# Aligned pads in SBUF and a new order of the first block's loads and tiles in a split-fp32 transformer layer

## The chip, the core and the metric

The kernel runs on one core of a Trainium2 chip. The core has a matrix engine (TensorE, PE in the profile; PEld is its loading of the stationary operand), VectorE (DVE), ScalarE (ACT), GpSimd (POOL) and SyncE (SP), which here issues nearly all transfers, and 16 DMA engines. Operands lie in SBUF, 128 partitions wide; TensorE accumulates into PSUM banks. The metric is the device time of one execution in microseconds; a comparison uses the median of several runs.

## What is computed

One layer over 2048 prompt tokens and 128 sample tokens (8 streams of 16), model width 1024, all in fp32:

```python
qm, km, vm, om, ip, fp, qa, ka, va = split_in(x @ w_in)          # 1024 -> 2824
...
hm, C1, n1, m1 = mlstm_chunkwise(qm, km, vm, logi, logf, C0, n0, m0, mchunk)
hm = (og * head_norm(hm, g_mlstm_norm)).reshape(B, T, M_WIDTH).astype(x.dtype)
qa = rope(qa.reshape(B, T, A_Q_HEADS, A_HEAD_DIM), pos)
ka = rope(ka.reshape(B, T, A_KV_HEADS, A_HEAD_DIM), pos)
...
mix = jnp.concatenate([hm, ha], axis=-1) @ w_out
h = layer_norm(DEEPNORM_ALPHA * x + mix, ln1_g, ln1_b)
f, conv_rows = conv_ffn(h, conv_prev, w_up, w_conv, b_conv, w_down)   # 1024 -> 5632 -> 2816 -> 1024
y = layer_norm(DEEPNORM_ALPHA * h + f, ln2_g, ln2_b)
```

The gates ip, fp and the keys and values ka, va make up 264 columns of the input projection; the other 2560 are five groups of 512.

## The kernel before

**How a product is made.** Every fp32 operand is split in two: a high half, made by a cast on ScalarE, and a low half, source minus high half, on VectorE (`split`, lines 217 and 218 for weights, 562 and 563 for x). TensorE multiplies high by high, high by low and low by high and adds them in PSUM. On top of it the large matrix products use a scheme of seven quadrant products in place of eight, so sums and differences of quadrants of x and of the weights have to be formed on VectorE first (`x_steps` for x, steps named t1 to t4, and `split_first` for the weights of the first block), and the results are combined after (`i_after`).

**Stages.** The input projection (`i_dense`) runs in four blocks of four tiles of 128 tokens, the first block with the sample tile as a fifth; it lies at 6 to some 655 us of the span, with mLSTM and attention steps of finished tiles woven in between. The output projection follows, then the up-projection with the convolution (line 1842 its matmuls, 384 or 320 columns wide, some 940 to 1890 us) and the down-projection with the last norm (line 2045, to the end).

**An order written by hand.** TensorE executes in the order of the program, which is a list of items, made in `i_begin`. An item ("p", b, g, s) is product s (1 to 7) of group g in block b: 24 matmuls of 256 columns (line 700), and in the first block, for s of 1, 2, 5 and 4, 12 more for the sample tile (line 710, PSUM tile psx). An item ("t", b, i, e) is a direct tile: the 264 columns for tile i of block b, 24 matmuls of 264 columns (line 726), not done by quadrants. For groups 0 and 1 the split x (`oh`, `ol`) is the moving operand and the weights stationary; for the later ones, as in the direct tiles, it is the other way round. Before, block 0 runs tiles 2, 3 and 4 first, then products (0,0,1), (0,0,2), (0,1,1), (0,0,7), (0,0,6), (0,0,5) and on; tiles 0 and 1 come at the block's end, ahead of tiles 2 and 3 of block 1, whose x is loaded and split during the last group.

**Loads and splits.** The weights and x come by DMA, issued from SP in program order. `next_raw` issues the next weight load if one of four raw slots is free; `next_split` splits the oldest loaded one into halves; `advance` does either as long as it can. A quadrant of weights or x is 512 KB. `x_load(0, q)` loads quadrant q of block 0's x: 1 and 3 hold the two halves of the model width for tiles 0 and 1, 2 and 4 those for tiles 2 and 3 (called x1 to x4 below; product 1 uses x1, product 2 uses x3, direct tiles 2 and 3 use x2 and x4); `xs` is the sample tile. The order of loads before is x2, the four parts of the 264 columns' weights (`wg`, 264 KB each), x4, xs, the rotary tables, x1, four quadrants of group 0, x3, a quadrant of group 1. Some sums of weight quadrants are kept in DRAM (`zws`) for the later blocks.

**After a direct tile** (`i_keys`): ScalarE copies keys, values and gates out of PSUM, VectorE turns the keys (rotary steps, lines 864 to 867), SP stores them. When all tiles of a block have their gates, `gate_logs` computes the log-sigmoid in sixteen small VectorE operations; in block 0 that is after tile 1, thus after the block's end, and block 1's first x splits are issued there too.

**Addresses.** Pools are laid out one behind the other in a partition. In the kernel before, the x tiles and their halves (pool `xp`) begin at 96 bytes past a multiple of 512, the up-projection's inputs (`hh1` to `hh7`, `hl1` to `hl7`, made in `f_tokens`) at 480, 96 or 128, the down-projection's features at 480 and 96. The weight halves begin at 192 and 320.

Of the kernel before, what the change touches and what calls it, by code (L numbers as in the profile page):

```python
# [14 lines left out]
P = 128  # L15
# [189 lines left out]
class Prog:  # L205
# [8 lines left out]

    def split(self, hi, lo, src):
        nc = self.nc
        nc.scalar.copy(hi, src)  # L217
        nc.vector.tensor_sub(lo, src, hi.bitcast(F32))  # L218
# [7 lines left out]
    def run(self):  # L226
        PS = bass.MemoryType.PSUM
        nb = len(OBLOCKS)
        with ExitStack() as es:
# [20 lines left out]
            wx, wxcm = enter("wx1sb")  # L250
            self.unit_more(wx)
# [31 lines left out]
            self.wx, wxcm = enter("wx2sb")  # L283
            self.f2, f2cm = enter("f2sb")
            self.f3, f3cm = enter("f3sb")
            self.f_ups(n)
            close(f3cm)
# [47 lines left out]
    def i_begin(self):  # L335
# [3 lines left out]
        for b in range(nb):  # L339
            if b == 0:  # L340
                it += [("t", 0, i, -1) for i in (2, 3, 4)]
                it += [("p", 0, 0, s) for s in (1, 2)] + [("p", 0, 1, 1)] + [("p", 0, 0, s) for s in (7, 6)]
# [16 lines left out]
            it += [("t", b, i, b) for i in (0, 1)]  # L359
# [60 lines left out]
    def next_raw(self):  # L420
# [5 lines left out]
        there = u[0] == "p" and u[1] == 0 and (u[2] == 0 and u[3] != 1 or u[3] in (5, 4, 3) or u[2:] == (1, 1))  # L426
        if not there and not self.kept(u) and not self.raw_free():
            return False
# [24 lines left out]
        elif u[0] == "g":  # L453
            self.raw_of[u] = e = self.raw_slot([P, 2, 264])
# [36 lines left out]
    def split_first(self, g, s, hi, lo):  # L491
# [9 lines left out]
        if s == 7:  # L501
            V.tensor_sub(r[a11], r[a11], r[a21])
            keep(a11, 7)
        elif s == 6:
# [3 lines left out]
            keep(a11, 6)  # L508
        q = {1: a11, 7: a11, 6: a11, 2: a12, 3: a12, 5: a21, 4: a22}[s]
# [5 lines left out]
        if g >= KEPT and s in SUMS:  # L515
            for i, t in enumerate((hi, lo)):
                nc.sync.dma_start(self.zws[g][SUMS.index(s)][i].rearrange("p a b -> p (a b)"), t.bitcast(F32))
        if s == (6 if g == 0 else 2):
# [17 lines left out]
    def x_steps(self, b, *steps):  # L536
# [3 lines left out]
        for s in steps:  # L540
# [14 lines left out]
            else:  # L555
# [3 lines left out]
                n = 4 if (b, s) == (0, "b12") else 1  # L559
# [18 lines left out]
    def i_first_weights(self):  # L578
        for q in ((0, 0), (1, 0), (1, 1), (0, 1)):
            self.raw_of[0, q] = self.raw_slot([P, 4, HT])  # L580
        for q in ((0, 0), (0, 1), (1, 0), (1, 1)):
            self.nc.sync.dma_start(self.raw_of[0, q][0], self.a["wi"][0][q])

    def i_dense(self):
# [3 lines left out]

        self.next_raw()
        self.x_load(0, 2)  # L590
        for _ in range(3):
            self.next_raw()
        self.x_load(0, 4)
        self.single_raw = self.tp.tile([P, KD, P], F32, name="xsr", tag="pth", bufs=2)
        nc.sync.dma_start(self.single_raw, a["xs"])
        self.angles = {}
        self.rope_load(IBLOCKS[0][2], 2)
        self.rope_load(NPT, 1)
        self.next_split()
        self.x_steps(0, "b12")  # L600
        for _ in range(3):
            self.next_split()
        self.x_steps(0, 3)
# [1533 lines left out]
```

## Time and profile before

| | us |
|---|---|
| median of 3 runs | 2361.76 (2360.01 to 2362.44) |
| the profiled execution | 2359.6 |
| its span | 2357.8 |
| TensorE busy | 2316.6 |
| VectorE busy | 1805.4 |
| ScalarE busy | 1297.9 |

The mean granted clock of TensorE is 0.997. The span is what lies between the first and the last recorded instruction. In a group's row the name left of the arrow is the tile written, those to its right the tiles read (for a matmul the moving operand and then the stationary one); then come the shapes, the count, the busy time and the mean duration of one, and the idle time ahead of it with what ended it. A matmul's duration is longer than the distance from one start to the next, because matmuls overlap; for a stream of them the distance counts. In a timeline row the first two numbers are start and length.

### The profile page before, as it was taken

How to read it: one execution, taken by the hardware profiler on the slowest of the kernel's cores; microseconds unless marked ns; L12 is line 12 of the kernel's file. 1: busy time of each engine (PE TensorE's matmuls, PEld its weight loads, DVE VectorE, ACT ScalarE, POOL GpSimd, SP SyncE). 2: the span in 40 equal slices, each digit the busy share in tenths (PEclk: the TensorE clock that was granted, in tenths of full speed). 3: DMA queues.
4: the chain of work that ended last, by engine and by line, in shares of the span. 5: the costliest groups of instructions: out<-in, count | busy, mean ns of one | idle time of the engine just before them, and what ended most of it. 6: DMA issues, size and time to landing. Idle time of an engine off the chain costs nothing.

```text
span 2357.8 us, 39882 instructions
## 1 busy us (share of the span) xinstructions
PE 2316.6 (98%) x14425; PEld 2123.4 (90%) x14425; DVE 1805.4 (77%) x3150; ACT 1297.9 (55%) x2465; POOL 243.4 (10%) x298
## 2 busy tenths in 40 slices
PE   8999999999999999999999999999999999999998
PEld 7999998999987777999999999999999978888876
DVE  8677586796678888987788677768766776795897
ACT  5353466676666664655556555555554544554643
POOL 0101101101212221300001000002100100000100
PEclk9999999999999999999999999999999999999999
DMA  7788899889977657787777989887988786757653
GB/s 278 263 308 291 282 290 313 285 289 319 301 259 247 210 208 251 264 324 277 281 270 252 309 314 318 303 271 263 321 286 265 230 283 203 240 186 226 233 181 108
DMA packets 296933, 624.98 MB, mean 265 GB/s; under 512 B 47004, under 2 KB 140192, under 8 KB 296736
## 3 DMA queue, kind: packets, MB, share of 16 engines
q1 hardware_dynamic: 295872, 619.29, 77.3%
q10 hardware_dynamic: 864, 3.15, 0.4%
q8 instruction: 114, 1.87, 0.3%
q14 instruction: 83, 0.68, 0.1%
HBM read 451.78 MB, written 170.56 MB: 264 GB/s over the span
## 4 chain that ended last, share of the span: by engine, by line
PE 73%; DVE 5%; DMA 2%; issue 2%; ACT 2%; POOL 0%; SPq 0%; DVEq 0%; ACTq 0%; POOLq 0%
PE dps L1842 18%; PE fup L1842 18%; PE dps L700 7%; PE dps L2045 7%; PE fht L2045 6%; PE fup L2045 6%; PE dps L222 2%; PE dps L224 2%; PE dps L223 2%; PE ppo L1337 1%; PE psc L1288 1%; PE ppt L1331 1%; PE dps L726 1%; DVE w L218 1%; DVE hl L218 1%
## 5 line engine op out<-in xcount | busy, mean ns | idle before, releaser
L1842 PE MATMUL dps<-hh,uw 128*128 128x384 f32 (+1 forms) x1848 | 481.0, 329 | 6.7 <-ACT u L1867 1.9
L1842 PE MATMUL fup<-hh,uw 128*128 128x384 f32 (+1 forms) x1848 | 479.8, 328 | 2.7 <-ACT u L1867 2.6
L1842 PEld LDWEIGHTS dps<-hh,uw 128*128 128x128 f32 x1848 | 330.0, 188 | 10.5 <-ACT u L1867 2.7
L1890 DVE SCALAR_TENSOR_TENSOR cc<-u,cw,cc 128x768 f32<-128x768 f32 (+1 forms) x264 | 252.4, 977 | 107.5 <-ACT cc L1888 105.5
L1842 PEld LDWEIGHTS fup<-hh,uw 128*128 128x128 f32 x1848 | 330.1, 188 | 4.0 <-ACT u L1867 3.5
L1842 PE MATMUL fup<-hl,uw 128*128 128x384 f32 (+1 forms) x924 | 302.8, 328 | 1.6 <-DVE hl L218 1.6
L1842 PE MATMUL dps<-hl,uw 128*128 128x384 f32 (+1 forms) x924 | 302.4, 327 | 0.0
L700 PE MATMUL dps<-w,oh 128*128 128x256 f32 x1344 | 259.3, 286 | 2.8 <-ACT zev L759 1.0
L218 DVE TENSOR_TENSOR w<-wraw,w 128x1024 fp32r<-128x1024 f32 (+2 forms) x167 | 190.4, 1148 | 58.8 <-ACT w L217 58.1
L217 ACT CAST w<-wraw 128x1024 fp32r<-128x1024 f32 (+2 forms) x167 | 163.0, 985 | 129.1 <-PE dps L700 52.9
L217 ACT CAST uw<-wraw 128x1024 fp32r<-128x1024 f32 x126 | 122.9, 978 | 189.3 <-PE dps L2045 108.8
L700 PEld LDWEIGHTS dps<-w,oh 128*128 128x128 f32 x1344 | 213.1, 189 | 14.7 <-issue 8.9
L1888 ACT ACTIVATE cc<-u,cw 128x768 f32<-128x768 f32 (+1 forms) x132 | 129.6, 998 | 123.0 <-DVE u L1881 61.4
L218 DVE TENSOR_TENSOR uw<-wraw,uw 128x1024 fp32r<-128x1024 f32 x126 | 142.4, 1132 | 71.0 <-ACT uw L217 70.2
L700 PE MATMUL dps<-w,ol 128*128 128x256 f32 x672 | 189.6, 282 | 0.0
L700 PE MATMUL dps<-oh,w 128*128 128x256 f32 x896 | 171.1, 285 | 8.2 <-ACT dps L775 2.9
L1842 PEld LDWEIGHTS fup<-hl,uw 128*128 128x128 f32 x924 | 173.6, 188 | 2.5 <-DVE hl L218 2.5
L2045 PE MATMUL fup<-uw,fu 128*128 128x512 f32 x726 | 174.1, 396 | 1.6 <-DVE uw L218 1.6
L1842 PEld LDWEIGHTS dps<-hl,uw 128*128 128x128 f32 x924 | 173.6, 188 | 0.0
L2045 PEld LDWEIGHTS fup<-uw,fu 128*128 128x128 f32 x726 | 136.3, 188 | 34.9 <-DVE uw L218 2.1
L2045 PE MATMUL dps<-uw,fu 128*128 128x512 f32 x660 | 165.0, 396 | 0.0
L700 PEld LDWEIGHTS dps<-oh,w 128*128 128x128 f32 x896 | 140.9, 188 | 14.7 <-issue 4.1
(331 smaller groups left out, 4624.7 us busy)
## 6 DMA issues: line engine op xcount, KB each, us to landing
uw<-zw SPq DMA_DIRECT2D x176, 512.0 KB, 4.9
zw<-uw SPq DMA_DIRECT2D x88, 512.0 KB, 2.9
w<-zws SPq DMA_DIRECT2D x72, 512.0 KB, 6.6
wv<-wup SPq DMA_DIRECT2D x66, 512.0 KB, 5.5
wraw<-wi SPq DMA_DIRECT2D x65, 512.0 KB, 4.9
wraw<-zt SPq DMA_DIRECT2D x60, 512.0 KB, 4.1
wraw<-wdn SPq DMA_DIRECT2D x45, 512.0 KB, 3.7
wraw<-wo SPq DMA_DIRECT2D x40, 512.0 KB, 4.5
```

The costliest lines, as they stand in the source:

```text
L217: nc.scalar.copy(hi, src)
L218: nc.vector.tensor_sub(lo, src, hi.bitcast(F32))
L222: mm(out, ah, bh, start=start, stop=False)
L223: mm(out, ah, bl, start=False, stop=False)
L224: mm(out, al, bh, start=False, stop=stop)
L700: mm(o, l, r, start=s in (1, 7) and c == k == i == 0, stop=k == 3 and i == 2, skip_group_check=True)
L726: mm(o, x, w, start=k == i == 0, stop=k == KD - 1 and i == 2, skip_group_check=True)
L1288: nc.tensor.matmul(ps[kvh][:, j, :nk], q[rs, j0 + j], k[rs, sel], start=i == 0, stop=i == 2)
L1842: mm(ps, l[:, k], r[:, k], start=s in (1, 7) and k == 0 and i == 0, stop=k == 3 and i == 2, skip_group_check=True)
L1888: S.activation(c[:, v], u[:, v, 2:2 + n], AF.Identity, bias=w[3], scale=w[2])
L1890: V.scalar_tensor_tensor(c[:, v], u[:, v, i:i + n], w[i], c[:, v], op0=ALU.mult, op1=ALU.add)
L2045: mm(ps, l[:, k, c], r[:, k], start=s in (1, 4, 7) and u == 0 and k == 0 and i == 0, stop=u == nu - 1 and k == n - 1 and i == 2, skip_grou ...
```

## The change

It has two parts that do not depend on each other.

The first is the head. Block 0 now begins with products (0,0,1), (0,0,2) and (0,1,1); all five direct tiles follow, 0 to 4, then (0,0,7) and (0,0,6), and none is left at the block's end. The loads are issued in the order of that use: x1 and the first weight quadrant in halves by turns, the first half of the sample tile, the second quadrant, x3, the other half of the sample tile, group 1's quadrant, wg0, wg1, x2, wg2, wg3, x4 and the last two quadrants; the raw wg go to slots of the x pool (`oh5`, `ol5`, `oh6`, `ol6`) that are not needed yet. x1 is split in quarters, in place of x2. The first product does the first half of the inner dimension for both column halves before the second. The sums of group 0's weight quadrants for products 5 and 6 are formed after product 7's split, not ahead of product 6's. Steps that hung on tile 1 of block 0 (splits of x for block 1, the gate steps) are moved to other items.

The second is the addresses: `skew` allocates a tile that nothing writes or reads, ahead of or between pools, so that what follows begins at a multiple of 512 bytes. The small tiles of the norms are taken from another pool (`f2` in place of `wp`). The number of instructions of each engine stays, but for three more DMAs on SP.

```diff
+    def skew(self, pool, n):
+        pool.tile([P, n // 4], F32, name="skew", tag=f"skew{n}", bufs=1)
+
...
             wx, wxcm = enter("wx1sb")
+            self.skew(wx, 64)
             self.unit_more(wx)
...
             self.wx, wxcm = enter("wx2sb")
+            self.skew(self.wx, 64)
...
             self.f_ups(n)
+            self.skew(self.f2, 480)
+            self.skew(self.wx, 448)
...
-                it += [("t", 0, i, -1) for i in (2, 3, 4)]
-                it += [("p", 0, 0, s) for s in (1, 2)] + [("p", 0, 1, 1)] + [("p", 0, 0, s) for s in (7, 6)]
+                it += [("p", 0, 0, s) for s in (1, 2)] + [("p", 0, 1, 1)]
+                it += [("t", 0, i, -1) for i in (0, 1, 2, 3, 4)] + [("p", 0, 0, s) for s in (7, 6)]
...
-            it += [("t", b, i, b) for i in (0, 1)]
+            if b:
+                it += [("t", b, i, b) for i in (0, 1)]
...
         there = u[0] == "p" and u[1] == 0 and (u[2] == 0 and u[3] != 1 or u[3] in (5, 4, 3) or u[2:] == (1, 1))
+        there = there or u[:2] == ("g", -1)
...
-            self.raw_of[u] = e = self.raw_slot([P, 2, 264])
+            if u[1] < 0:
+                e = [self.xp.tile([P, 2, 264], F32, name="graw", tag=("oh5", "ol5", "oh6", "ol6")[u[2]], bufs=1), False]
+            else:
+                e = self.raw_slot([P, 2, 264])
+            self.raw_of[u] = e
             nc.sync.dma_start(e[0], a["wg"][u[2]])
...
-        if s == 7:
-            V.tensor_sub(r[a11], r[a11], r[a21])
-            keep(a11, 7)
-        elif s == 6:
+        def sums():
             V.tensor_add(r[a21], r[a21], r[a22])
             keep(a21, 5)
             V.tensor_sub(r[a11], r[a22], r[a11])
             keep(a11, 6)
+        if s == 7:
+            V.tensor_sub(r[a11], r[a11], r[a21])
+            keep(a11, 7)
+        elif s == 6 and g:
+            sums()
...
+        if s == 7 and g == 0:
+            sums()
...
-                n = 4 if (b, s) == (0, "b12") else 1
+                n = 4 if (b, s) == (0, 1) else 1
...
-        for q in ((0, 0), (0, 1), (1, 0), (1, 1)):
-            self.nc.sync.dma_start(self.raw_of[0, q][0], self.a["wi"][0][q])
...
+        def quad(*q):
+            nc.sync.dma_start(self.raw_of[0, q][0], a["wi"][0][q])
+
         self.next_raw()
-        self.x_load(0, 2)
-        for _ in range(3):
-            self.next_raw()
-        self.x_load(0, 4)
+        first, x1 = self.raw_of[0, (0, 0)][0], self.x_raw(1)
+        self.xr[0, 1] = x1
+        for k in (slice(0, 2), slice(2, 4)):
+            nc.sync.dma_start(first[:, k], a["wi"][0][0, 0][:, k])
+            nc.sync.dma_start(x1[:, k], a["xq"][0][0, 0][:, k])
         self.single_raw = self.tp.tile([P, KD, P], F32, name="xsr", tag="pth", bufs=2)
-        nc.sync.dma_start(self.single_raw, a["xs"])
+        nc.sync.dma_start(self.single_raw[:, :4], a["xs"][:, :4])
+        quad(0, 1)
+        self.x_load(0, 3)
+        nc.sync.dma_start(self.single_raw[:, 4:], a["xs"][:, 4:])
+        for q in (2, 4):
+            for _ in range(2 + (q == 2) * 2):
+                self.next_raw()
+            self.x_load(0, q)
+        quad(1, 0)
+        quad(1, 1)
         self.angles = {}
+        self.rope_load(IBLOCKS[0][0], 2)
         self.rope_load(IBLOCKS[0][2], 2)
         self.rope_load(NPT, 1)
         self.next_split()
-        self.x_steps(0, "b12")
-        for _ in range(3):
-            self.next_split()
-        self.x_steps(0, 3)
-        self.x_single(1, 2)
-        self.x_load(0, 1)
-        self.next_raw()
-        self.x_load(0, 3)
         self.x_steps(0, 1)
-        self.advance()
-        self.x_steps(0, 2, "t3", 7, "t2", 6)
-        self.x_single(4)
-        self.x_steps(0, "t1", 5, "t4")
+        self.x_single(1)
+        self.next_split()
+        self.x_steps(0, 2)
+        self.x_single(2)
+        self.next_split()
+        begin = {("p", 0, 0, 1): ["b12"], ("p", 0, 0, 2): [3], ("p", 0, 1, 1): ["t3", 7],
+                 ("t", 0, 0, -1): ["t2", 6], ("t", 0, 2, -1): ["t1", 5, "t4"]}
...
-                ps = self.bank([P, 512], "pg") if ti == 4 else self.ib[ti % 2 * 2]
+                ps = self.bank([P, 512], "pg") if ti == 4 or e < 0 and ti % 2 == 0 else self.ib[ti % 2 * 2]
                 yield from self.i_direct(b, ti, e, ps)
                 self.i_keys(b, ti, ps)
-                if ti == 1:
+                if ti == 1 and b:
                     if b + 1 < nb:
                         self.x_steps(b + 1, 1, 2)
...
                     after = [6, b + 1]
                 elif ti == 3 and b or ti == 4:
                     self.release(4)
+                elif item in begin:
+                    self.x_steps(0, *begin[item])
+                if ti == 3 and b or ti == 4:
                     self.x_steps(b, 4)
...
-            if (g, s) == (1, 6):
+            if b and (g, s) == (1, 6):
...
+            if (b, g, s) == (0, last, 4):
+                self.x_steps(1, 1, 2)
+                after = [6, 1]
...
             with self.tc.issue_after(behind) if behind and b == 0 else nullcontext():
                 self.advance()
+                self.x_steps(0, *begin.get(item, ()))
+                if item == ("p", 0, 0, 2):
+                    self.x_single(4)
...
-        for c in range(2):
+        pairs = [(0, 0), (1, 0), (0, 2), (1, 2)] if (b, g, s) == (0, 0, 1) else [(0, 0), (0, 2), (1, 0), (1, 2)]
+        for c, k0 in pairs:
             m = slice(c * P, c * P + P)
             o = ps[:, c * HT:(c + 1) * HT]
-            for k in range(4):
+            for k in (k0, k0 + 1):
                 for i, (w, x) in enumerate(((wh, hh), (wh, hl), (wl, hh))):
...
-                if k % 2:
-                    yield 645
+            yield 645
...
-        one = lambda n, w: self.wp.tile([P, w], F32, name=n, tag=n, bufs=3)
+        one = lambda n, w: self.f2.tile([P, w], F32, name=n, tag=n, bufs=3)
...
+        self.skew(self.fp, 480)
```

## The prediction

> **What bounds the kernel now.** I read first the page's busy times and two of its groups, then the busy time by stretch (us from the start, length, then busy us and count of PE, PEld, DVE, ACT and POOL, granted clock, DMA share and GB/s), then the head's timeline.
>
> ```profile
> PE 2316.6 (98%) x14425; PEld 2123.4 (90%) x14425; DVE 1805.4 (77%) x3150; ACT 1297.9 (55%) x2465; POOL 243.4 (10%) x298
> ...
> L700 PE MATMUL dps<-w,oh 128*128 128x256 f32 x1344 | 259.3, 286 | 2.8 <-ACT zev L759 1.0
> ...
> L700 PE MATMUL dps<-oh,w 128*128 128x256 f32 x896 | 171.1, 285 | 8.2 <-ACT dps L775 2.9
> ```
>
> ```profile
> 0.00:6.00 6.00, 4.03 (x10) 2.87 (x10) 2.38 (x12) 2.42 (x4) 0.31 (x5) 1.00 0.66 206
> 6.00:11.00 5.00, 2.95 (x14) 2.23 (x14) 4.04 (x8) 3.89 (x8) 0.00 (x0) 0.95 0.99 385
> 11.00:17.00 6.00, 5.55 (x25) 5.24 (x25) 4.76 (x9) 3.48 (x9) 0.00 (x0) 0.50 1.02 411
> 17.00:21.50 4.50, 4.50 (x38) 4.50 (x38) 3.78 (x10) 2.02 (x6) 0.00 (x0) 0.97 0.57 221
> 21.50:28.70 7.20, 4.34 (x37) 4.13 (x36) 7.20 (x9) 5.86 (x8) 0.00 (x0) 1.00 0.41 132
> 28.70:45.00 16.30, 14.70 (x120) 14.29 (x120) 15.55 (x20) 6.76 (x8) 0.00 (x0) 1.00 0.77 267
> 45.00:51.00 6.00, 4.86 (x38) 4.66 (x39) 4.19 (x4) 2.06 (x3) 0.00 (x0) 1.00 0.84 330
> ...
> 950.00:1890.00 940.00, 930.36 (x5636) 923.15 (x5636) 716.69 (x961) 510.41 (x874) 84.89 (x178) 1.00 0.82 284
> 1890.00:2357.80 467.80, 458.34 (x1963) 368.11 (x1961) 364.98 (x460) 232.68 (x313) 24.57 (x17) 1.00 0.62 207
> ```
>
> TensorE is busy 98% of the span, so only two things can pay: fewer idle or slowed microseconds on it, or a shorter time per matmul. In the two feed-forward stretches (the last two rows) it idles 9.6 us of 940 and 9.5 of 468. The head is different. Until 17 us the DMA engines are full (0.99 and 1.02 of their time at 385 and 411 GB/s), the granted clock falls to 0.50 between 11 and 17 us, and from 21.5 to 45 us VectorE works 22.75 of 23.5 us while TensorE idles 4.5. The head waits first for bytes, then for VectorE.
>
> The timeline of the head, TensorE, ScalarE and VectorE:
>
> ```profile
> 4.61 0.41 ACT L562 CAST oh<-xr 128x256 fp32r<-128x256 f32 x1 [2.60 <-DMA xr<-xq]
> ```
> ```profile
> 5.05 0.43 DVE L563 TENSOR_TENSOR ol<-xr,oh 128x256 fp32r<-128x256 f32 x1 [2.23 <-ACT oh L562]
> ```
> ```profile
> 1.97 4.21 PE L325 MATMUL dps<-zero 128*128 128x512 f32 x9 [1.97 <-DVE zero L320]
> ...
> 18.54 3.07 PE L726 MATMUL pg<-w,xs 128*128 128x264 f32 x24
> ...
> 21.45 0.28 PE L700 MATMUL dps<-oh,w 128*128 128x256 f32 x1
> ...
> 24.26 1.57 PE L710 MATMUL psx<-w,xs 128*128 128x256 f32 x12
> ...
> 28.70 0.38 PE L700 MATMUL dps<-oh,w 128*128 128x256 f32 x1 [2.87 <-ACT dps L775]
> ...
> 34.80 0.50 PE L700 MATMUL dps<-oh,w 128*128 128x256 f32 x2 [1.32 <-DVE w L218]
> ```
> ```profile
> 44.82 0.60 ACT L767 ACTIVATE zev<-dps 128x512 f32<-128x512 f32 x1 [1.90 <-PE dps L700]
> ```
>
> A direct tile of 24 matmuls takes 21.45 - 18.54 = 2.91 us; a product's 24 take 24.26 - 21.45 = 2.81; the 12 for the sample tile half of that, 1.41. The fifth product, (0,0,6), is over when ScalarE starts its copy at 44.82.
>
> **The head, part by part.** Up to the end of (0,0,6) the old order runs three direct tiles, five products and three sample groups; the new one runs two direct tiles more, taken from the end of the block. So I compare the end of (0,0,6) and credit the two tiles, 2 x 2.91 = 5.8 us, because the block's end is shorter by them.
>
> When can the new order begin? The old kernel moved 1.24 MB by 6 us (206 GB/s x 6) and 3.16 MB by 11 us. Its first x load was cast from 4.61. The new order sends x1 and the first weight quadrant in halves, 1.05 MB together: by those rates their last byte moves at about 5.4 us, their first half well before. So the first product starts when the warm-up on zeros ends, 1.97 + 4.21 = 6.2 us; its second half, with about 1 us to the cast and 0.41 + 0.43 us for each quarter, comes about in time (0 to 0.7 us late; I take 0.3). The second product needs x3, which lies behind x1, the quadrant, the first half of xs and another quadrant: 2.36 MB, moved at about 8.9 us, landed at about 10; a whole cast is 1.05 us and its subtraction 1.23, so its low half is there at 12.4. By then product 1 and its sample group have ended at 6.2 + 0.3 + 2.81 + 1.41 = 10.7. That is a new wait of 1.7 us in place of the old direct tiles' waits for x and weights. All later loads (0.5 MB each 1.25 us) come before their turn: the third product's weights near 12, wg0 to wg3 and x2 by 16, x4 by 17.5, against direct tiles that start at about 20.8.
>
> Work to the end of (0,0,6): 5 products 14.05, 3 sample groups 4.23, 5 direct tiles 14.55, sum 32.8 us. End = 6.2 + 32.8 + 0.3 + 1.7 = 41.0 us. Gain = 44.8 - 41.0 + 5.8 = 9.6 us. Of it, 2.5 us and a little at the edges is the clock: the 25 matmuls of the 11 to 17 us row kept TensorE busy 5.55 us, where 25 x 0.121 = 3.0. The rest is the idle time of the rows above: the 2.87 and 1.32 us waits for the casts of products 2 and 3 go, since five direct tiles now stand where VectorE catches up.
>
> Given back first at product (0,0,5), where the 45 to 51 us row has 1.14 us of idle time. VectorE is busy some 35 us of the 40 from 5.05 to 45.0 (4.04, 4.76, 3.78, 7.20 and 15.55). The new head adds the rotary steps of two tiles (four small instructions, about 1.0 us a tile) and, after t4, block 0's gate steps, sixteen small ones, which I put at 0.2 us each. VectorE is through at 4.7 + 35.3 + 2.0 = 42.0 us if it never idles, and at 46.6 if it idles 4.6 us as now, 49.8 with all gate steps ahead too, against TensorE's 41.0. Net of the wait that is there already the loss is between -1.1 and 7.7 us; most of the early idling goes with the loads' order, and the last products' splits stand ahead of the gate steps, so I take 1.4. SP's three additional half loads, some 0.4 us of issue each, stand ahead of full DMA engines: nothing. The extra sums (moved from product 6 to 7) are the same instructions on VectorE.
>
> Given back again at the block's end. Timeline there, TensorE, then VectorE:
>
> ```profile
> 158.80 0.40 PE L726 MATMUL dps<-w,oh 128*128 128x264 f32 x2
> ```
> ```profile
> 164.65 0.41 PE L726 MATMUL dps<-w,oh 128*128 128x264 f32 x2
> ```
> ```profile
> 157.89 1.23 DVE L218 TENSOR_TENSOR w<-wraw,w 128x1024 fp32r<-128x1024 f32 x1 [2.95 <-ACT w L217]
> ...
> 162.20 1.22 DVE L563 TENSOR_TENSOR ol<-xr,oh 128x1024 fp32r<-128x1024 f32 x1
> ```
>
> From 158.80 to 164.65 TensorE runs t0 and t1; behind that cover VectorE runs three operations of 0.7 to 1.2 us between the two shown, for block 1's x and a last copy. The next tile, (1,2), needs low halves that end at 163.4, 1.2 us before its turn. Without the cover it begins at 158.8, and if VectorE's chain stays where it is relative to the last product, its second matmul waits 4.6 us. The chain starts late only because VectorE idled 2.95 us for a weight load, and the copies of two tiles are no longer between; if that slack closes entirely the wait is nothing. I take 2.7, a little over the middle. Behind this wait stand all of TensorE's later matmuls. After it the order of TensorE's instructions is the same as before to the end, and every later wait I found is on work that moves with it.
>
> Sum of the head: 9.6 - 1.4 - 2.7 = 5.5 us gained, with ends of -2.7 (9.6 - 7.7 - 4.6) and 10.7. If a clock drop comes back in the new head it costs about the same 2.5 us.
>
> A rule bears on that. The Trainium skill, "TensorE: Matmul & The Clock Gate", section "What's actually happening", says that the array falls to half clock after an idle window of about 3.4 us and is released by a busy one. Here the clock fell near 10.5 us although TensorE had 2.95 busy us in 6 to 11, and stayed at 1.00 over the 2.87 us idle before 28.70: the trace agrees only in part. By the rule the new 1.7 us wait would cost no clock.
>
> **The addresses.** The padding moves x, its casts, the features and the down-projection's inputs from offsets 96, 128 and 480 (mod 512 bytes, from the compiled kernels) to 0. No instruction is added; the pads are never written. The norm's small tiles move to another pool: nothing. What could change is a matmul's pace. Against it: the products read the cast x (offset 96) as moving operand in the page's second L700 group and weights (offsets 192, 320) in the first, and the mean durations are 285 and 286 ns. Per column: 2.91 us / (24 x 264) = 0.459 ns in a direct tile, 2.81 / (24 x 256) = 0.457 in a product. For it: within L1842 the pace differs by place.
>
> ```profile
> 956.97 0.34 PE L1842 MATMUL fup<-hh,uw 128*128 128x384 f32 x1
> ...
> 958.70 0.34 PE L1842 MATMUL fup<-hl,uw 128*128 128x384 f32 x1
> ```
> ```profile
> 1099.89 0.34 PE L1842 MATMUL fup<-hh,uw 128*128 128x384 f32 x1
> ...
> 1101.66 0.34 PE L1842 MATMUL fup<-hl,uw 128*128 128x384 f32 x1
> ```
>
> Ten matmuls start from the first to the last of each pair: 173 ns each in one place, 177 in the other, 2.3% apart, at unaligned addresses both. What sets this is unknown. The work one of whose operands (moving, or stationary in the down-projection and in the later products) changes its address is about 930 + 458 us of the stretches above and 3360 product matmuls of 0.117 us (393 us), 1780 us together. With the mean taken midway, all at the good pace would gain 1.15%, 20 us, and all at the bad one would lose as much. Products from several offsets agree, so I take 0.
>
> **Sum.** 5.5 us off the profiled 2359.6 (span 2357.8 and 1.8 around it) is 2354.1; that execution was 2.2 under the median, so 2361.8 - 5.5 = 2356.3. Forecast 2356, chance 0.45, own range 2351 to 2361.
>
> **Rivals.** (1) The gain is swallowed: VectorE's lateness at (0,0,5) and the new wait at the block's end are near their dear ends, or the clock falls. For it: VectorE 97% busy from 21.5 to 45 us. Time 2362, with the head's two losses at 5 and 4.6 us, within 0.2%. Chance 0.09. (2) Slower: the new addresses put more matmuls at the bad pace. It decides from 0.6% on the 1780 us (10.2 us: the head's 5.5 are used up and 4.7 more are lost); midway from there to all of 20 us it is +15 - 5.5, 2371. For it the 177 ns row, against it the equal means of L700. Chance 0.21, of it 0.18 slower by over 0.2%. (3) The new addresses put them at the good pace: half of 20 us and the head, 2346. For it the 173 ns row. Chance 0.15. (4) Nothing is given back, VectorE keeping up because the five direct tiles let it: 9.6 us, 2352. For it the cover of 14.6 us; against it the 1.2 us slack at 164.65. Chance 0.10.
>
> **How the numbers follow.** A difference of under 0.2%, 4.7 us, can't be told from none here. The forecast lies just past it: I count 0.30 of its 0.45 as faster and 0.15 as the same. Faster 0.30 + 0.15 + 0.10 = 0.55; same 0.15 + 0.09 + 0.03 = 0.27; slower 0.18. The range 2344 to 2367 holds the forecast, rivals 1, 3 and 4, and the mild half of 2.
>
> **What would show it.** Right: L700 before L726 on TensorE, its first matmul near 6.2 us; a wait of 1 to 2.5 us before the second product; no 2.87 us wait for L775; a clock of 1.00 through the head; (0,0,6) over near 41; a new wait of some 2 to 4.5 us at the first direct tiles of block 1, near 156 us; equal stretches and busy times from there on. Wrong: a clock of 0.50 anywhere before 20 us, product 2 later than 13.5, no wait at the block's end, or TensorE's busy time in L1842 off by over 3 us for the same 5544 matmuls, which would be the addresses' doing.

## The result, and the profile after

| | before | after |
|---|---|---|
| median, us | 2360.37 (2356.30 to 2362.44, 5 runs) | 2347.06 (2345.55 to 2353.46, 5 runs) |
| ratio, 95% interval | | 0.9949 (0.9938 to 0.9961) |
| profiled execution, us | 2359.6 | 2345.55 |
| its span, us | 2357.8 | 2343.8 |

The changed kernel is 0.51% faster, about 12 us by the ratio and 13 by the medians. Busy time by stretch of the kernel after, with the columns and the stretches of the prediction:

```profile
0.00:6.00 6.00, 4.03 (x11) 2.99 (x11) 2.73 (x13) 2.40 (x4) 0.31 (x5) 1.00 0.59 161
6.00:11.00 5.00, 2.79 (x11) 2.30 (x11) 2.78 (x8) 2.96 (x7) 0.00 (x0) 0.74 0.99 354
11.00:17.00 6.00, 6.00 (x51) 6.00 (x50) 5.66 (x7) 5.01 (x8) 0.00 (x0) 0.93 1.04 415
17.00:21.50 4.50, 4.50 (x41) 4.50 (x40) 3.82 (x6) 3.55 (x5) 0.00 (x0) 1.00 0.93 354
21.50:28.70 7.20, 7.20 (x62) 7.20 (x61) 7.20 (x8) 2.56 (x5) 0.00 (x0) 1.00 0.40 143
28.70:45.00 16.30, 15.61 (x132) 15.42 (x131) 16.30 (x30) 9.35 (x16) 0.00 (x0) 1.00 0.78 243
45.00:51.00 6.00, 4.89 (x42) 4.68 (x41) 5.68 (x18) 1.85 (x3) 0.00 (x0) 1.00 0.88 291
...
950.00:1890.00 940.00, 930.35 (x5625) 921.30 (x5624) 711.92 (x957) 507.77 (x869) 77.71 (x178) 1.00 0.82 283
```

From 11 to 43 us TensorE now hardly idles, where the kernel before idled 4.5 us between 21.5 and 45. The clock still falls: it is 0.74 from 6 to 11 us and 0.93 from 11 to 17. The up-projection's stretch has the same busy time as before (930.35 against 930.36 us), but where TensorE hardly waits, the busy time of a fixed stretch can't show a change of pace. The number of matmuls that start in it can. A stretch of the down-projection without any wait, 240 us of the kernel before and then of the kernel after,

```profile
1990.00:2230.00 240.00, 240.00 (x1030) 193.18 (x1030) 184.53 (x224) 129.38 (x173) 15.17 (x10) 1.00 0.67 218
```

```profile
1990.00:2230.00 240.00, 240.00 (x1042) 195.18 (x1041) 190.90 (x235) 133.71 (x181) 18.86 (x12) 1.00 0.68 223
```

holds 1030 matmuls of 512 columns before (233.0 ns each) and 1042 after (230.3 ns). The clock is 1.00 in both and neither waits. The instructions are the same; only addresses differ. That is 2.7 ns on each of 1980 matmuls, 5.3 us.

Where the order's part stands is read from one matmul that both kernels have: the first of product (1,0,1), behind block 1's first two direct tiles. TensorE's timeline, before and then after:

```profile
170.51 0.28 PE L700 MATMUL dps<-oh,w 128*128 128x256 f32 x1
```

```profile
1.98 3.72 PE L332 MATMUL dps<-zero 128*128 128x512 f32 x9 [1.98 <-DVE zero L327]
5.60 0.39 PE L734 MATMUL dps<-oh,w 128*128 128x256 f32 x1
...
8.66 0.58 PE L734 MATMUL dps<-oh,w 128*128 128x256 f32 x1 [2.21 <-ACT oh L579]
...
12.79 1.58 PE L743 MATMUL psx<-w,xs 128*128 128x256 f32 x12
14.21 0.28 PE L734 MATMUL dps<-oh,w 128*128 128x256 f32 x1
...
43.51 0.39 PE L734 MATMUL dps<-oh,w 128*128 128x256 f32 x1 [0.69 <-ACT zev L800]
...
49.08 0.39 PE L734 MATMUL dps<-oh,w 128*128 128x256 f32 x1 [1.11 <-DVE zev L804]
...
157.29 0.51 PE L759 MATMUL dps<-w,oh 128*128 128x264 f32 x2 [0.27 <-ACT oh L579]
160.47 0.39 PE L759 MATMUL dps<-w,ol 128*128 128x264 f32 x1 [2.67 <-DVE ol L580]
...
167.70 0.28 PE L734 MATMUL dps<-oh,w 128*128 128x256 f32 x1
```

Block 1's first direct tile begins 7.4 us earlier than before (157.29 against 164.65), waits at once, and 10 us later the lead is down to 2.8 us (167.70 against 170.51). VectorE's timeline after shows why:

```profile
156.33 1.22 DVE L580 TENSOR_TENSOR ol<-xr,oh 128x1024 fp32r<-128x1024 f32 x1 [0.21 <-ACT oh L579]
157.47 0.68 DVE L806 TENSOR_TENSOR zev<-dps,zev 128x512 f32<-128x512 f32 x1
158.07 1.21 DVE L567 TENSOR_TENSOR xr<-xr,wraw 128x1024 f32<-128x1024 f32 x1
159.21 1.22 DVE L580 TENSOR_TENSOR ol<-xr,oh 128x1024 fp32r<-128x1024 f32 x1
```

It is the chain that the prediction quoted, in the same order, about 3 us earlier, and TensorE stands before its last step. Behind the wait the clock is halved for 3.41 us (the first row is the stretch ahead of it, with the wait):

```profile
158.57:161.99 3.42, 1.51 (x12) 1.52 (x13) 3.42 (x4) 0.10 (x1) 0.00 (x0) 1.00 0.74 211
161.99:165.40 3.41, 3.41 (x18) 3.41 (x18) 2.26 (x4) 1.49 (x3) 0.00 (x0) 0.50 1.01 371
```

A direct tile's matmul takes 0.121 us at full clock, so 28 fit into 3.41 us; here the row counts 18, those that only overlap its ends included. Of the 4.6 us of lead lost between 157.29 and 167.70, 2.9 are the wait and its first 0.27, and about 1.7, half of 3.41, the clock.

### The profile page after: what moved, and what is told of

Same layout as the page of the kernel before. It is cut to its first block, busy times and chain, and to the rows that moved or that the text cites. A ratio compares the mean times of both kernels' runs of the same rounds, so it can differ in the third digit from the quotient of the medians.

```text
span 2343.8 us, 39880 instructions
## 1 busy us (share of the span) xinstructions
PE 2304.7 (98%) x14425; PEld 2116.7 (90%) x14425; DVE 1805.6 (77%) x3150; ACT 1298.6 (55%) x2465; POOL 244.7 (10%) x298
## 4 chain that ended last, share of the span: by engine, by line
PE 72%; DVE 6%; DMA 2%; issue 2%; ACT 2%; POOL 0%; SPq 0%; DVEq 0%; ACTq 0%; POOLq 0%
PE fup L1875 18%; PE dps L1875 18%; PE dps L2079 6%; PE dps L734 6%; PE fup L2079 6%; PE fht L2079 5%; PE dps L225 2%; PE dps L227 2%; PE dps L226 2%; PE ppo L1370 1%; PE psc L1321 1%; PE ppt L1364 1%; PE dps L759 1%; DVE hl L221 1%; DVE w L221 1%
```

## The experiments

Theory: the order and the addresses gain separately; the order loses most of its lead at the end of block 0, and the addresses gain through the pace of matmuls. Rivals: one of the two makes all of it.

**The order alone.** All `skew` calls removed and the norm's tiles put back.

```diff
-            self.skew(wx, 64)
...
-        one = lambda n, w: self.f2.tile([P, w], F32, name=n, tag=n, bufs=3)
+        one = lambda n, w: self.wp.tile([P, w], F32, name=n, tag=n, bufs=3)
...
-        self.skew(self.fp, 480)
```

> The new order of the first block with the old addresses. Theory (two separate gains: the order is worth what it has gained by the end of block 0, 4.3 us in the traces, and the addresses the rest, through the pace of matmuls): 4 to 6 us under the kernel before, a ratio of 0.9975 to 0.9983; the waits of the changed kernel at 8.7 and 160 us and the half clock behind both are there, the 512-column matmuls of the down-projection still start 233.3 ns apart. Rival (the order makes the whole difference, and the later one is how runs vary): 12 to 14 us under it. Rival (the order gains nothing in the end, since the block's end gives it back): no difference.

Measured: 2356.87 us (12 runs) against 2360.38, ratio 0.9990 (0.9981 to 0.9998). The first matmul of (1,0,1), in TensorE's timeline of this run, and the stretch of the down-projection:

```profile
169.23 0.28 PE L730 MATMUL dps<-oh,w 128*128 128x256 f32 x1
```

```profile
1990.00:2230.00 240.00, 240.00 (x1030) 193.16 (x1029) 185.86 (x227) 131.47 (x177) 16.94 (x12) 1.00 0.67 218
```

By 169 us 1.3 us of lead are left, and the down-projection is that of before to the matmul. The order is worth 0.5 to 4.5 us by the ratio's interval, somewhat under what was expected. The rival that the order makes the whole difference is out, the one that it gains nothing only just.

The half clock behind the first wait was not there as expected. In this run's trace TensorE is slow from its start on:

```profile
5.98 0.41 PE L730 MATMUL dps<-oh,w 128*128 128x256 f32 x1
...
8.54 0.58 PE L730 MATMUL dps<-oh,w 128*128 128x256 f32 x1 [1.72 <-ACT oh L575]
...
15.61 0.28 PE L730 MATMUL dps<-oh,w 128*128 128x256 f32 x1
```

Up to 15 us its matmuls of 256 columns start 0.21 us apart in place of 0.12 (the trace has no record of the clock before 15.02 us, and the profile then shows 1.00). The last row, product 2, starts at 15.61 us, 1.4 us after the changed kernel's 14.21. So nearly all of the difference between 1.3 and 2.8 us of lead is the clock at the start of these two executions, and not the addresses.

**The addresses alone.** The kernel before with the same `skew` calls and the norm's tiles in `f2`.

```diff
...
+        self.skew(self.fp, 480)
         self.in_down = True
```

> The new addresses with the old order. Theory: 7 to 9 us under the kernel before; the down-projection's matmuls start about 230.8 ns apart in place of 233.3 (4.8 us over 1980), the 256-column products about 115.8 in place of 116.8 (3.4 us over 3360), the up-projection's 384-column ones within 0.3 ns; the head is the old one, with its wait of 2.9 us. Rival (addresses make no difference): within 2 us of the kernel before. Rival (addresses make all of it): 12 us or more under it.

Measured: 2349.69 us (6 runs) against 2360.38, ratio 0.9958 (0.9945 to 0.9971), about 10 us, a little over the theory's 7 to 9. The rival that addresses make no difference is out; 12 us or more is still inside the interval (6.8 to 13 us), and it is the order's own run that speaks against it. Its down-projection is that of the changed kernel, with the old head:

```profile
1990.00:2230.00 240.00, 240.00 (x1042) 195.17 (x1041) 188.66 (x230) 133.96 (x180) 18.85 (x12) 1.00 0.67 221
```

Together the two parts give 3.5 + 10.7 = 14.2 us by medians, against 13.3 measured together. By stage, in us, from one trace of each kernel:

| | first matmul of the up-projection at | from there to the down-projection's first | from there to its last matmul |
|---|---|---|---|
| before | 941.2 | 944.4 | 464.1 |
| order alone | 938.5 | 943.9 | 464.2 |
| addresses alone | 935.5 | 946.3 | 459.0 |
| changed | 934.0 | 942.9 | 459.0 |

The addresses gain 5.2 us in the down-projection, alike with either order, and some 3 to 6 us ahead of the up-projection, where the 256-column products are (5.7 with the old order; 4.5 with the new one, of which 1.5 is the clock at the start). The up-projection differs by a few us from trace to trace and shows no gain that goes with the addresses. What the norm's tiles in `f2` do by themselves was not tried.

**Is it the multiple of 512, or the distance to the other operand?** In the kernel before the 1980 matmuls fall apart by the address of the weights (their moving operand), and in the changed kernel they do so too, but otherwise. All features begin at 480 before; the weights lie in eight buffers at 64, 192, 320 and 448 and in two more at 96 before and at 64 after. Means from start to start, ns, worked out from the traces with the addresses of the compiled kernels:

| weights at (mod 512) | features at 480 (before) | at 0 (after) | at 128 | at 256 |
|---|---|---|---|---|
| 64 | 234.4 | 229.4 | 233.5 | 229.4 |
| 96 | 232.7 | - | - | - |
| 320 | 234.3 | 230.0 | 232.1 | 229.9 |
| 192 | 233.0 | 232.8 | 230.7 | 232.9 |
| 448 | 232.6 | 232.2 | 229.0 | 232.2 |
| mean of all | 233.4 | 230.7 | 231.8 | 230.7 |

The last two columns are experiments that move the pool of the features, to 128 (below) and to 256 (224 in place of 352).

```diff
-        self.skew(self.fp, 480)
+        self.skew(self.fp, 352)
```

> The changed kernel with the pool of the down-projection's features (and of three up-projection inputs) moved by 128 bytes, so that they begin at 128 past a multiple of 512; the weights stay at 192, 320, 448 and 64. Theory (what counts is the distance between the moving and the stationary operand, modulo 256): the down-projection's matmuls start 230 to 231.5 ns apart as in the changed kernel, but those with weights at 192 and 448 become the fast ones (229.4) and those at 64 and 320 the slow ones (232.4). Rival (what counts is that the features begin on a multiple of 512): back to 233 to 234 for all, 4.8 us lost.

> The same pool moved by 256 bytes. Theory (distance modulo 256): as the changed kernel, 230 to 231.5 ns, those with weights at 64 and 320 the fast ones. Rival (a multiple of 512 counts): 233 to 234 for all, 4.8 us lost.

At 128 the fast and the slow buffers change places; at 256 all is as at 0. The single runs took 2350.24 and 2346.17 us. At 128 the mean is 0.3 ns beyond the expected 231.5, because the two extra buffers also lie at 64, on the slow side now: 231.8 where an even count had been assumed. So a multiple of 512 isn't needed: for these matmuls the distance between moving and stationary operand modulo 256 counts, and 64 is better than 192, 96 or 224. It isn't all: pairs at one distance still differ by up to 1.7 ns here (229.0 and 230.7 at 64).

**The pairs by themselves.** Behind the changed kernel, groups of 24 matmuls on zeros.

```diff
+        for busy in (0, 1):
+            for w in (512, 384, 256):
+                for m, s in [(m, 0) for m in (0, 64, 128, 192, 256, 384)] + [(0, s) for s in (32, 64, 96, 128, 192, 480)]:
...
+                    for n in range(24):
+                        k = n % 3 * 128 + s // 4
+                        self.nc.tensor.matmul(ps[:, :w], sta[:, k:k + 128], mov[:, m // 4:m // 4 + w], start=n == 0, stop=n == 23, skip_group_check=True)
```

> The changed kernel, and behind its end 72 groups of 24 matmuls on zeros, of 512, 384 and 256 columns, with the moving tile's start at 0 to 384 bytes past a multiple of 512 and the stationary one's at 0 to 480, once with the other engines idle and once with casts on ScalarE and subtractions on VectorE beside them. The output is that of the changed kernel. Theory (the pace follows from where the moving and the stationary operand lie against each other, TensorE by itself): groups of one width differ by 1 to 5 ns (0.5 to 2%) from pair to pair, alike in both passes. Rival (it follows from other engines' and DMA traffic in SBUF): all pairs alike in the idle pass, near 219 ns for 512 columns, and 3 to 8% slower in the busy one.

The two passes agreed to 0.1 ns in 35 of the 36 pairs (the first group began at half clock). Two groups of 512 columns, moving operand at 64 and at 128 and the stationary one at 0, first pass and then second (a stretch runs from the group's first start to the next group's first):

```profile
2361.79:2367.30 5.51, 5.51 (x25) 4.51 (x24) 5.37 (x5) 0.17 (x1) 0.00 (x0) 1.00 0.00 0
2367.30:2372.89 5.59, 5.59 (x26) 4.53 (x25) 5.42 (x6) 0.17 (x1) 0.00 (x0) 1.00 0.01 3
2512.84:2518.35 5.51, 5.51 (x25) 4.51 (x24) 0.00 (x0) 2.27 (x3) 0.00 (x0) 1.00 0.00 0
2518.35:2523.94 5.59, 5.59 (x26) 4.52 (x24) 0.00 (x0) 2.27 (x3) 0.00 (x0) 1.00 0.00 0
```

The first pass wasn't idle as meant: VectorE's subtractions ran in most of it, ScalarE's casts in the second. Neither changed a group by more than 0.1 ns. So the pace follows the pair and not the work of these two engines; DMA traffic was next to none in both passes. The second set has all sixteen pairs.

```diff
+                for m, s in [(0, 0)] + [(m, s) for m in (0, 64, 128, 192) for s in (0, 64, 128, 192)]:
```

> The changed kernel and behind it groups of 24 matmuls on zeros for all pairs of the phases 0, 64, 128 and 192 of the moving and the stationary tile, at 512, 384 and 256 columns. Theory (the distance modulo 256 alone sets the pace): the four pairs at one distance agree within 0.5 ns; 512 columns take 227.6 ns at distance 0, 229 at 64, 233 to 234 at 128 and 192. Rival (each address counts by itself): pairs at one distance differ by over 1 ns.

Start to start, ns, by the distance moving minus stationary modulo 256 (each the range over its four pairs):

```
distance      0              64             128            192
512 columns   226.7 - 227.6  229.2 - 229.4  232.2 - 232.3  233.3 - 233.4
384 columns   173.3 - 174.3  173.1 - 173.8  175.7 - 176.1  176.7 - 177.0
256 columns   119.7 - 120.2  117.7 - 117.8  118.3 - 118.7  113.5 - 117.8
```

In the profile, the groups of 512 columns with the moving tile at 0 and the stationary one at 0, 64, 128 and 192:

```profile
2353.88:2359.32 5.44, 5.44 (x26) 4.50 (x24) 0.00 (x0) 0.17 (x1) 0.00 (x0) 1.00 0.00 0
2359.32:2364.92 5.60, 5.60 (x26) 4.51 (x25) 0.00 (x0) 0.17 (x1) 0.00 (x0) 1.00 0.01 3
2364.92:2370.49 5.57, 5.57 (x25) 4.52 (x24) 0.00 (x0) 0.17 (x1) 0.00 (x0) 1.00 0.00 0
2370.49:2376.00 5.51, 5.51 (x25) 4.51 (x24) 0.00 (x0) 0.17 (x1) 0.00 (x0) 1.00 0.00 0
```

For 512 columns the distance is the rule, to 0.9 ns. The best distance is not the same for every width: equal phase is the fastest at 512 columns and the slowest at 256. For 256 one pair stands alone: (64, 128) took 113.5 ns and the other three at that distance 117.8, while the earlier set had 113.5 at (0, 64). For 384 the earlier set had 173.2 at (192, 0) where this one has 177.0. There something besides the two phases counts; what it is stays open.

**Put to use.** Every weight buffer at one phase modulo 256 (an offset of 128 bytes in every other one) and the features at that phase.

```diff
+        o = 32 if n % 2 == phase else 0
+        return self.wp.tile([P, 1056], dt, name=name, tag=tag, bufs=1)[:, o:o + 1024]
...
-        self.skew(self.fp, 480)
+        self.skew(self.fp, 288)
```

> The changed kernel with every buffer of weight halves placed at one phase modulo 256: 64 in the projections before the feed-forward, 192 in the feed-forward (by an offset of 128 bytes inside every other buffer), and the down-projection's features at 192 too, so that its moving and stationary operands begin at the same phase. Theory (the pace of a width follows from the two phases, as the groups on zeros have it: 512 columns 227.6 ns at equal phase, 228.9 to 229.7 at 64 apart, 233 to 234 else; 384 columns 173.2 at 64 apart and 174 at equal phase; 256 columns 113.5 with the moving operand at 0 and the stationary one at 64, else about 118): the down-projection goes from 230.7 to about 227.6, 6 us; the other three kinds give 5 to 6 us more; 2334 to 2339. Rival (the zeros' table doesn't carry over to the kernel's own data and other traffic): within 3 us of the changed kernel.

Measured: 2340.92 us, ratio to before 0.9921 (0.9907 to 0.9934), 6 us under the changed kernel. The down-projection holds 1059 matmuls in the same 240 us, 226.6 ns each:

```profile
1990.00:2230.00 240.00, 240.00 (x1059) 198.28 (x1058) 194.13 (x238) 135.19 (x183) 18.86 (x12) 1.00 0.68 226
```

The zeros' value for equal phases carries over to real data with the DMA engines 68% busy. The whole down-projection takes 453.5 us against 459.0, about the 6 us expected of it. In the up-projection the 384-column matmuls 64 apart take 173.1 ns, as on zeros, and those at equal phase 175.4, about 1 ns more than there (means of the distances under 250 ns). The other three kinds, put at 5 to 6 us, gave next to nothing: the up-projection begins at 934.5 us (934.0 in the changed kernel) and takes 943.8 (942.9), and the products' mean is 116.1 ns against 116.2, since their 3 us rested on the lone 113.5 ns pair. So the run is some 2 us over the expected 2334 to 2339.

**The wait at the end of block 0.** The quadrant whose low half is late (b12) gets a slot that is free one product earlier and is split there.

```diff
-                self.hx[b, s] = h, l = self.x_slot(4 if s == "b12" else s)
+                self.hx[b, s] = h, l = self.x_slot((5 if b else 4) if s == "b12" else s)
...
-        passages = [{..., 3: [3, "t4"], 4: ["b12", "t1"]}, ...]
+        passages = [{..., 3: ["b12", 3, "t4"], 4: ["t1"]}, ...]
```

> The changed kernel, with the x quadrant that tiles 2 and 3 of the next block need first (b12) split one product earlier, into a slot that is free by then. Theory (the new wait at the block's end is for this split's low half, queued on VectorE behind other work, and the half clock behind it costs as much again as half of it): the wait of 2.7 us at 160 us and the half clock after it go, 3 to 4.4 us under the changed kernel, about 2343. Rival (something else is late next, the weights of the direct tiles or the next x split): under 1.5 us gained, with a new wait there.

Measured: 2344.58 us (2341.68 to 2348.39), ratio to before 0.9936 (0.9923 to 0.9949); 2.5 us under the changed kernel by medians, intervals overlapping. TensorE's timeline:

```profile
162.44 0.28 PE L734 MATMUL dps<-oh,w 128*128 128x256 f32 x1
```

```profile
333.76 0.58 PE L734 MATMUL dps<-oh,w 128*128 128x256 f32 x1 [4.17 <-ACT zev L792]
```

The wait and its half clock are gone: (1,0,1) starts at 162.44, 5.3 us before the changed kernel's 167.70 (0.7 of them were there when the first direct tile began). At 334 us a wait of 4.17 us takes back part of it, where the changed kernel has two of 0.9 and 1.5 us, and around its end the clock is halved for 6.83 us, where the changed kernel's is 1.00:

```profile
333.07:339.90 6.83, 6.14 (x28) 6.14 (x29) 5.88 (x20) 3.12 (x7) 1.93 (x1) 0.50 1.05 357
```

So the early split was tried in block 0 alone:

> The changed kernel with the early split of b12 at the end of block 0 alone; blocks 1 to 3 as in the changed kernel. In the run with the early split in every block the wait at block 0's end went (3.7 us by there) and a wait of 4.2 us came up at 334 us, where the changed kernel has 0.9 and 1.5 us. Theory (that wait comes from the later blocks' moved splits): it stays at the changed kernel's 2.4 us and the gain is 3 to 4.5 us under the changed kernel, 2343. Rival (it comes from the whole program running earlier against the attention steps woven in): a wait of 3 to 4 us about 334 us is there again, 2 to 2.5 us gained, about 2344.6.

Measured: 2345.63 us (2342.17 to 2348.43), ratio 0.9934 (0.9921 to 0.9948). The 4.2 us wait didn't come back (0.92 and 1.23 us there), as the theory had it, but neither the theory's 3 to 4.5 us nor the rival's 2 to 2.5 came of it: this time a wait at 50 us was 2.59 us in place of 1.11, with the same instructions in the same order up to there:

```profile
50.12 0.58 PE L734 MATMUL dps<-oh,w 128*128 128x256 f32 x1 [2.59 <-DVE zev L804]
```

The 0.58 us of its first matmul (0.39 elsewhere) is half clock again. The two runs with the early split are 1.4 and 2.5 us under the changed kernel by medians, which their intervals don't tell from nothing.

**The first product.** In the changed kernel it runs 3 matmuls, waits 2.21 us for x1's second quarter and goes on at half clock. ScalarE casts that quarter only after a weight cast that waits for a landing. Here the splits of x and weights are issued quarter by quarter, on top of the early split.

```diff
             self.split(hi[:, c], lo[:, c], f[:, c])
+            if n > 1:
+                k = slice(i, i + 1)
+                nc.scalar.copy(xh[:, k], x[:, k])
+                V.tensor_sub(xl[:, k], x[:, k], xh[:, k].bitcast(F32))
```

> The same, and the splits of the first quadrant of x and of weights issued by turns, quarter by quarter. In the changed kernel ScalarE's cast of x's second quarter stands behind a weight cast that waits for the second half's landing (7.59 us), so TensorE has 3 matmuls to do and then waits 2.2 us, at half clock behind it. Theory: 9 more matmuls run before the second half lands, and the first product ends 1 to 2 us sooner: 4 to 6 us under the changed kernel, about 2341.5. Rival (the landing of the second half sets the head, and VectorE afterwards): no more than 0.5 us beyond the run with the early split alone.

Measured: 2345.64 us, ratio 0.9944 (0.9931 to 0.9957), nothing beyond the early split alone. TensorE's waits in its head:

```profile
8.88 0.39 PE L740 MATMUL dps<-oh,w 128*128 128x256 f32 x1 [0.79 <-ACT oh L535]
...
14.17 0.38 PE L740 MATMUL dps<-ol,w 128*128 128x256 f32 x1 [0.88 <-DVE ol L587]
...
43.46 0.39 PE L740 MATMUL dps<-oh,w 128*128 128x256 f32 x1 [0.69 <-ACT zev L806]
```

The 2.21 us wait went, and the clock stayed at 1.00 from 7 us on, yet product 2 gets its low half at 14.17 (14.21 was its start in the changed kernel) and the wait at 43.5 us is where it was. x3 lands at 11.6 us here and at 11.4 in the changed kernel, and its cast begins within 0.3 us in both. So the landing of x3 sets the head; what is saved ahead of it becomes a wait for it. The rival held.

**All that helped, together.** The even weights and block 0's early split.

> The same, with the early split of b12 at block 0's end. Theory: another 1 to 3 us, about 2334, since the wait at 160 us and its half clock go and some of it comes back as later waits. Rival (a faster TensorE before that point is late by as much more): no difference to the run without it.

Measured: 2339.55 us, ratio to before 0.9906 (0.9891 to 0.9921): the lowest median here, 7.5 us under the changed kernel, though not told apart from the even weights alone; the 2334 expected didn't come.

## Why the prediction was right, and where it wasn't

The sign and the range held. The likeliest case, 2356, lay 9 us too high, and 2347 is outside its own 2351 to 2361; what came is nearest to the third rival, which had a chance of 0.15 and 2346 forecast for it. That the number fits so well is in part luck. The rival rested on the up-projection's 173 and 177 ns rows, and the up-projection gained nothing; its 10 us were half of a bound. The gain came from the down-projection and the products, and the order gave less than the 5.5 us added to it. Of the signs that the prediction named for being wrong, two were there: the clock at 0.50 before 20 us, and product 2 later than 13.5 us (14.21).

- **The step that failed is the addresses, taken as 0.** They are worth about 10 us, 5.2 of them in the down-projection. The prediction had seen two paces at one width, and weighed against it the equal means of two groups (285 and 286 ns). But each such group mixes pairs from four weight buffers (at 64, 192, 320 and 448, not at two addresses as had been read), good and bad, so that equal means said nothing of a pair. The address of one operand isn't the variable; the distance between the two is, wholly so for 512 columns and in part for the others. The work listed as exposed was right. The bound of 1.15% either way holds for this change in the down-projection, 1.1% (233.4 to 230.7), but is no bound for addresses: with the even weights it is 2.8% (226.8). The products gained 1 to 2 ns of 118 (118.3 to 116.2 in the mean of all distances under 150 ns), the up-projection next to nothing (175.35 to 175.18 for 384 columns), since there the new pairs are half better and half not.
- **The head up to (0,0,6).** Expected end 41.0 us, measured 42.86, when ScalarE's copy starts (its timeline after):

```profile
42.86 0.60 ACT L800 ACTIVATE zev<-dps 128x512 f32<-128x512 f32 x1 [1.73 <-PE dps L734]
```

  The first matmul came earlier (5.60 against 6.2), because in this execution the clock rose during the warm-up (nine matmuls in 3.72 us, 4.21 before); that is luck. The first product's second half came much later (8.66, with 2.21 us of wait against 0.3) and at half clock, and x3's low half, done at 13.75, about 1.3 us later than 12.4. The wait of 1.7 us ahead of product 2 didn't come as such: the first product was late enough to hide it. Product 2 starts at 14.21 in place of 12.4, and from there all takes what was summed. The loads land later than rate times bytes says: 161 GB/s in the first 6 us, against 206 in the old order from which the estimate was made.
- **The wait at (0,0,5)** was sized 1.4 us; the two waits are 0.69 and 1.11 against 0.75 and 0.66 before, 0.4 us more. (The lower end of that loss, -1.1, should be -0.1 by the prediction's own 42.0 and 41.0; its 10.7 would be 9.7.)
- **The wait at the end of block 0** was right in place, cause and size (2.9 us against 2.7). What the sum lacked is the half clock behind it, about 1.7 us, and the same around the first wait. The prediction let 1.7 us cost no clock; a 2.2 us wait and a 2.9 us one did, and in the run with block 0's early split alone one of 1.43 us, over at 7.79, with the clock at 0.50 from 9.06.
- **The order's net:** 5.5 us expected, 2.8 and 1.3 us in the two traces by block 1's first product, 0.5 to 4.5 by the ratio. With the measured terms the prediction's own sum comes out: 44.8 - 42.9 + 5.8 - 0.4 - 2.9 - 1.7 = 2.7. Later waits move by one or two us from trace to trace: the 1.42 us one at 949 us is absent in the changed kernel's profile and in the order's alone, and back as 1.53 with the even weights. That part isn't the order's.

## What to carry to other kernels

When a change moves only addresses, compare the pace start to start, by pair of buffers, in a stretch without waits; a group's mean duration hides it. A tile that is moved away from the end of a block may have been the cover for the next block's preparation: price the wait that follows, and a half clock after it that may come or not. A gain of a few us in one trace can be the clock's: look first at where each trace has it halved. What is saved ahead of a fixed landing isn't saved.

## What the runs showed of the hardware that wasn't expected

TensorE's pace for 512 columns depends on where the two operands start against each other modulo 256 bytes: 226.7 to 227.6 ns at equal phase and 233.4 at 192, 3% apart, the same to 0.1 ns with VectorE or ScalarE busy beside it. The Trainium skill, "TensorE: Matmul & The Clock Gate", section "Back-to-back issue gap", gives N / 2.4 + 2.5 ns for the gap of a warm matmul by itself, which is an estimate of 215.8 for 512 columns. No pair of the groups on zeros came under 226.7, and that rule has no address in it. The measurement decides.

The clock fell to 0.50 in the changed kernel during the 2.2 us wait that ends at 8.66 (from 8.39) and after the 2.9 us one that ends at 160.47 (from 161.99). In the kernel before, 2.87 us of idle time ahead of 28.70 left it at 1.00. The Trainium skill, "TensorE: Matmul & The Clock Gate", section "What's actually happening", speaks of an idle window of about 3.4 us; both waits here that were followed by half clock were shorter. The length of the wait alone doesn't decide it here.

What does can be read from the traces' records of the clock. It stays halved for 3.41 us or a multiple of that, and within a trace all its changes lie whole multiples of 3.41 us apart (in the changed kernel it is halved from 8.39, 161.99, 264.38 and 291.69 us, and once more after the last matmul). Divided into stretches by this raster of 3.41 us, the changed kernel around its first wait, and then the kernel before around its 2.87 us wait:

```profile
4.97:8.39 3.42, 1.48 (x6) 0.73 (x5) 1.53 (x5) 1.51 (x5) 0.00 (x0) 1.00 0.93 285
8.39:11.80 3.41, 3.14 (x13) 2.91 (x14) 2.61 (x7) 2.76 (x6) 0.00 (x0) 0.50 1.03 414
```

```profile
24.13:27.54 3.41, 1.71 (x15) 1.50 (x13) 3.41 (x4) 3.12 (x4) 0.00 (x0) 1.00 0.65 217
27.54:30.95 3.41, 2.25 (x19) 2.25 (x19) 3.41 (x5) 2.16 (x3) 0.00 (x0) 1.00 0.38 85
```

The 2.87 us wait falls into two stretches, with 1.71 and 2.25 us of work. Over all 13 traces, the clock fell behind each of the 27 stretches at full clock in which TensorE was busy for less than 45% (1.54 us), behind 7 of 48 with 45 to 58%, and behind 16 of 8927 with more. Those 16 wait for nothing: they are full of matmuls of 64 columns. The clock fell behind all 14 stretches in which 21 or more of these start, behind 2 of 5 with 20, and behind none of 9 with 16 to 19. One or two of them lie between 258 and 295 us in every trace, as in the changed kernel:

```profile
260.97:264.38 3.41, 3.41 (x28) 2.48 (x27) 1.06 (x2) 0.37 (x1) 0.00 (x0) 1.00 0.91 316
264.38:267.80 3.42, 3.42 (x18) 3.17 (x17) 0.42 (x1) 0.00 (x0) 0.00 (x0) 0.50 0.24 78
```

Where the raster lies differs between executions, so that a wait of the same length costs about 1.7 us of clock in one and nothing in the next. With the features at 256 the wait at the end of block 0 is 2.67 us as in the changed kernel, but the raster divides it at 157.27 us, and the clock stays at 1.00:

```profile
158.75 0.39 PE L759 MATMUL dps<-w,ol 128*128 128x264 f32 x1 [2.67 <-DVE ol L580]
```

```profile
155.00:165.00 10.00, 7.08 (x56) 6.67 (x56) 8.88 (x12) 5.83 (x9) 0.00 (x0) 1.00 0.86 267
```

Why the clock falls behind matmuls of 64 columns was not tried.
